# A down projection taken from six groups of matmuls to seven block products, with the sums of its blocks formed in DRAM

## The chip, the cores and the metric

The kernel runs on one core of a Trainium2 chip (a core has TensorE, here PE; VectorE, DVE; ScalarE, ACT; GpSimd, POOL; and SyncE, SP, which only issues transfers). The metric is device time in microseconds, the median of the runs of one program.

## What is computed

Two layers of an encoder over 1024 tokens of width 1024: a mixer of three parallel head groups, a cross-attention to a memory of 256 tokens, and a gated feed-forward part of width 2816. Only the last is changed in what it multiplies:

```python
def conv_gated_ffn(h, w_up, conv_w, conv_b, w_down):
    a = h @ w_up
    ap = jnp.pad(a, ((0, 0), (1, 1), (0, 0)))
    a = ap[:, :-2] * conv_w[0] + ap[:, 1:-1] * conv_w[1] + ap[:, 2:] * conv_w[2] + conv_b
    gate, val = a[..., :D_FF], a[..., D_FF:]
    return (jax.nn.silu(gate) * val) @ w_down

for l in range(DEPTH):                       # DEPTH = 2
    x = x + hybrid_mixer(rms_norm(x, mix_norm[l]), ...)
    x = x + memory_cross_attention(rms_norm(x, mem_x_norm[l]), mem, ...)
    x = x + conv_gated_ffn(rms_norm(x, ffn_norm[l]), ffn_w_up[l], ffn_conv_w[l], ffn_conv_b[l], ffn_w_down[l])
return rms_norm(x, final_norm)
```

## The kernel before

The residual x stays in SBUF as eight tiles of 128 tokens. A product in float32 accuracy is three matmuls: each operand is split into a high part, rounded to the format that PE multiplies, and a low part, the rest, and high x high, high x low and low x high go into one bank of PSUM (`mm3`, L113 to L115). PSUM is eight banks: four single ones (`bank`) and two pairs (`pair`). SBUF beside x is 46 slots of 128 x 1024 words (`s` in the rows).

**Attention.** An item is one head and one half of the queries: 4 steps of scores, exponentials on ACT (L296), scaling by the sum on POOL (`scale`, L302), then transposes on PE (L137) whose results ACT and DVE split (L120, L121), then the product with the values. There are 24 items in a layer, and the transposes of one stand among the scores of the next.

**The up projection's sums of blocks.** The up projection already is seven products of blocks in place of eight. The sums of weight blocks that it needs are formed in DRAM during the attention: a copy of one block (`up_copy`, issued on ACT, L778) and, four items later, a transfer that adds another block to it (`up_add`, issued on POOL, L781). Two of the four sums add an earlier sum. 24 copies and 24 adds a layer are spread over 20 items. In the rows these tensors are `u`.

**The up projection.** 22 channel tiles j, seven products each of 12 matmuls (L1104 to L1106). A weight piece of 256 KB is fetched nine products ahead (L1050) and split four ahead (L1057 on ACT, L1058 on DVE). The gate and value of j then pass a convolution (L1144 to L1152) and are multiplied (`gate`, L1158); `keep` stores the tile of 128 channels x 1024 tokens to DRAM (L1162, tensor `g`).

**The down projection.** The 22 channel tiles are read back in six groups of 3, 4, 4, 4, 4, 3. `load_down` fetches the weight rows and the stored tile through SP (L103), takes the high parts on POOL (L107, weights) and ACT (L105, activations) and the low parts on DVE (L108). For each group, token tile and half of the 1024 output columns there is one bank with 3 matmuls for each channel tile, and DVE adds it to x (`add_to_x`, L366). In the last group the next layer's norm of each token tile follows (L142, L128, L129, L144), and the transposes of its first half of the tokens stand between the last tiles; at the end of the second layer the final norm and the output (L1272, L1274; `final_last` for the last tile, L1251 to L1264).

**The order.** The functions are called in the order of the code, and the framework places each engine's instructions from it by its own estimates of when buffers come free; an engine then executes its list strictly in that order. Calls under `tc.keep_in_program_order` stay where the code has them. A tile of PSUM can be taken only when the one before it in the same bank has had its last reader.

## Time and profile before

| | us |
|---|---|
| median of 3 runs | 2869.32 (2869.23 to 2872.6) |
| the profiled execution, its own time | 2875.77 |
| its span, first to last instruction | 2873.6 |
| PE busy in it | 2798.3 |
| mean granted clock | 0.994 |

The page of the profile tells busy time by engine, groups of instructions by line with the mean of one in nanoseconds, and transfers by queue. Where a row has `x1297 | 509.1, 392`, there were 1297 instructions, busy for 509.1 us, 392 ns each; what follows names the idle time before them and what ended it. The matmuls overlap each other, so a record of 392 ns is not the time that one costs.

### The profile page before, as it was taken

To read this page: it belongs to the slowest core of one execution; us is meant where nothing else is said; L and a number is where in the kernel's file an instruction comes from. 1 tells how busy PE (TensorE), PEld (TensorE's weight loads), DVE (VectorE), ACT (ScalarE), POOL (GpSimd) and SP (SyncE) were. 2 spreads that over 40 slices of the span, in tenths; PEclk is the share of its full clock that TensorE was granted. 3 is DMA by queue.
4 is the path that set the end of the run, shared out by engine and by line. 5 is a ranking of instruction groups with operands and counts; after the bars stand their busy time and mean duration, and the time that the engine had idled before them with its cause. 6 is when DMAs were issued, how large, how long until landed. Compare 5 with 4: busy or idle time off the path is not lost. (4 is left out here: it accounts for less than half of the span.)

```text
span 2873.6 us, 37125 instructions
## 1 busy us (share of the span) xinstructions
PE 2798.3 (97%) x13909; PEld 2344.1 (82%) x13909; DVE 1975.6 (69%) x2825; ACT 1341.3 (47%) x2572; POOL 660.9 (23%) x628
## 2 busy tenths in 40 slices
PE   9998999999999999999999989999999999999998
PEld 7987787788878888888889777878887888888887
DVE  5578888656687777864445788895667877778544
ACT  4377877224554444310133778772345544443101
POOL 3244566320000000210123345663200000002100
PEclk9999999999999999999999999999999999999999
DMA  4015676311133333531110157752221333335311
GB/s 145 23 51 131 170 176 133 88 61 64 45 110 132 122 121 131 183 133 51 38 46 23 60 135 178 175 130 66 68 65 45 125 122 122 131 126 189 110 59 59
DMA packets 93635, 297.61 MB, mean 104 GB/s; under 512 B 10384, under 2 KB 11024, under 8 KB 83216
## 3 DMA queue, kind: packets, MB, share of 16 engines
q1 hardware_dynamic: 79488, 202.70, 21.1%
q0 software_dynamic: 6912, 46.14, 8.8%
q10 hardware_dynamic: 7056, 46.40, 4.5%
q8 instruction: 110, 1.80, 0.2%
q14 instruction: 69, 0.57, 0.1%
HBM read 267.94 MB, written 119.54 MB: 135 GB/s over the span
## 5 line engine op out<-in xcount | busy, mean ns | idle before, releaser
L113 PE MATMUL bank<-s,s 128*128 128x512 f32 (+4 forms) x1831 | 678.8, 371 | 5.9 <-DVE s L124 2.6
L115 PE MATMUL bank<-s,s 128*128 128x512 f32 (+4 forms) x1831 | 676.1, 369 | 0.9 <-DVE s L124 0.5
L114 PE MATMUL bank<-s,s 128*128 128x512 f32 (+4 forms) x1831 | 674.3, 368 | 0.0
L107 POOL TENSOR_SCALAR s<-s 128x1024 fp32r<-128x1024 f32 (+1 forms) x114 | 142.8, 1257 | 1374.3 <-DMA s<-in_w_down 1007.7
L121 DVE TENSOR_TENSOR s<-bank,s 128x512 fp32r<-128x512 f32 (+3 forms) x552 | 332.7, 631 | 109.1 <-ACT s L120 106.8
L120 ACT ACTIVATE s<-bank 128x512 fp32r<-128x512 f32 (+3 forms) x552 | 288.3, 555 | 238.4 <-PE bank L137 165.8
L113 PEld LDWEIGHTS bank<-s,s 128*128 128x128 f32 x1831 | 345.5, 189 | 62.7 <-DVE s L121 3.7
L115 PEld LDWEIGHTS bank<-s,s 128*128 128x128 f32 x1831 | 346.2, 189 | 53.8 <-DVE s L124 1.6
L114 PEld LDWEIGHTS bank<-s,s 128*128 128x128 f32 x1831 | 346.3, 189 | 50.9
L137 PE MATMUL bank<-ident,s 128*128 128x128 f32 (+1 forms) x2320 | 327.8, 276 | 45.5 <-DVE s L121 37.0
L137 PEld LDWEIGHTS bank<-ident,s 128*128 128x128 f32 (+1 forms) x2320 | 271.6, 141 | 108.0 <-issue 32.6
L302 POOL TENSOR_SCALAR s<-s,stat 128x1024 f32<-128x1024 f32 x192 | 224.5, 1169 | 249.1 <-DVE stat L301 159.6
L366 DVE TENSOR_TENSOR x<-x,bank 128x512 f32<-128x512 f32 x214 | 145.6, 683 | 195.5 <-PE bank L115 195.1
L292 DVE TENSOR_REDUCE stat<-pair 128x1 f32<-128x1024 f32 x192 | 234.2, 1220 | 65.4 <-PE pair L734 38.0
L1105 PE MATMUL bank<-s,s 128*128 128x512 f32 x704 | 274.8, 390 | 0.9 <-DVE s L206 0.9
L1106 PE MATMUL bank<-s,s 128*128 128x512 f32 x704 | 274.2, 389 | 0.0
L1104 PE MATMUL bank<-s,s 128*128 128x512 f32 x704 | 274.0, 390 | 0.0
L1057 ACT ACTIVATE s<-s 128x512 fp32r<-128x512 f32 x308 | 187.9, 627 | 161.7 <-PE bank L1106 49.8
L108 DVE TENSOR_TENSOR s<-s,s 128x1024 fp32r<-128x1024 f32 (+4 forms) x172 | 217.4, 1274 | 59.8 <-POOL s L107 46.1
L296 ACT ACTIVATE s<-pair,stat 128x1024 f32<-128x1024 f32 x192 | 214.3, 1116 | 16.9 <-DVE stat L292 10.3
L1058 DVE TENSOR_TENSOR s<-s,s 128x512 fp32r<-128x512 f32 x308 | 201.3, 687 | 24.4 <-ACT s L1057 20.8
L1104 PE MATMUL pair<-s,s 128*128 128x512 f32 x528 | 208.5, 395 | 1.2 <-ACT s L208 1.0
(164 smaller groups left out, 4519.5 us busy)
## 6 DMA issues: line engine op xcount, KB each, us to landing
s<-u SPq DMA_DIRECT2D x176, 256.0 KB, 3.0
u<-in_w_up ACTq DMA_DIRECT2D x40, 1024.0 KB, 6.5
s<-in_w_up SPq DMA_DIRECT2D x132, 256.0 KB, 3.3
g<-s SPq DMA_DIRECT2D x44, 512.0 KB, 2.8
s<-in_w_down SPq DMA_DIRECT2D x44, 512.0 KB, 4.4
s<-g SPq DMA_DIRECT2D x44, 512.0 KB, 5.4
u<-in_w_up POOLq DMA_DIRECT2D x20, 1024.0 KB, 9.8
u<-u POOLq DMA_DIRECT2D x20, 1024.0 KB, 10.0
```

The costliest lines, as they stand in the source:

```text
L108: nc.vector.tensor_tensor(lo[:, :cols], raw[:, :cols], f(hi[:, :cols]), ALU.subtract)
L113: nc.tensor.matmul(o, l[0], r[0], start=first, stop=False)
L114: nc.tensor.matmul(o, l[0], r[1], start=False, stop=False)
L115: nc.tensor.matmul(o, l[1], r[0], start=False, stop=last)
L120: nc.scalar.activation(hi, src, AF.Copy)
L121: nc.vector.tensor_tensor(lo, src, f(hi), ALU.subtract)
L137: nc.tensor.transpose(b[:m, j * P : (j + 1) * P], s, ident)
L292: nc.vector.reduce_max(self.nm[:, 0:1], s, axis=AX.X, negate=True)
L302: nc.gpsimd.tensor_scalar(p, p, r[:, 0:1], 0.0, ALU.mult, ALU.add)
L1104: nc.tensor.matmul(o, lh, rh, start=k == 0 and m in (1, 5, 6), stop=False, skip_group_check=True)
L1105: nc.tensor.matmul(o, lh, rl, start=False, stop=False, skip_group_check=True)
L1106: nc.tensor.matmul(o, ll, rh, start=False, stop=k == 3, skip_group_check=True)
```

## The change

The down projection becomes seven products of blocks too. The two halves of the tokens, the two halves of the output columns, and even and odd channel tiles make blocks of 512 tokens x 1408 channels and 1408 channels x 512 columns. A product runs over all 11 channel tiles of its block in four banks, one for each token tile, and DVE adds or subtracts the four results to one quarter of x when the product ends, some of them after a further product was accumulated in the same bank. The order is 1, 5, 6, 3, 7, 2, 4; products 1, 6, 7 and 4 use the four single banks, from the first to the last without release, and 5, 3 and then 2 the two pairs.

The sums of weight blocks are formed as the up projection's, in the same 20 items: 36 copies and 36 adds a layer in place of 24. The sums of the activations' blocks are formed in DRAM as well: for a pair of channel tiles `keep` issues seven stores of 256 KB on SP and four adds on POOL. Each block of a product fetches one activation piece and one weight piece of 256 KB (L1194, L1195 of the changed kernel), and takes both high parts on ACT and both low parts on DVE.

The copies move from ACT's queue to SP's, and each is made to wait for the scaling on POOL that stands last before it in the code (`Item.last`), so that they don't all start at once. The last four blocks of product 4 are done tile by tile, so that norms or output can follow.

```diff
-FGROUPS = [3, 4, 4, 4, 4, 3]
+D_AHEAD, D_FETCH = 4, 8
+UP_PARTS, DOWN_PARTS = (2, 4, 4, 4, 4, 4), (3, 4, 4)
...
-            nc.gpsimd.tensor_scalar(p, p, r[:, 0:1], 0.0, ALU.mult, ALU.add)
+            Item.last = nc.gpsimd.tensor_scalar(p, p, r[:, 0:1], 0.0, ALU.mult, ALU.add)
...
-        def up_copy(m, i):
-            tc.keep_in_program_order(nc.scalar.dma_start(up_sum[m, i], up_piece({5: 2, 6: 0, 7: 0, 3: 1}[m], i)))
...
+            def copy(self, m, i):
+                c = nc.sync.dma_start(self.sum[m, i], self.piece({5: 2, 6: 0, 7: 0, 3: 1}[m], i))
+                tc.add_manual_dep(ins_of(c), ins_of(Item.last).name, mybir.DependencyInfo(mybir.DependencyClass.Sync, mybir.DependencyReason.DATA), reason="not sooner")
+
+            def add(self, m, i):
+                src = self.sum[{6: 5, 3: 6}[m], i] if m in (6, 3) else self.piece({5: 3, 7: 2}[m], i)
+                tc.keep_in_program_order(nc.gpsimd.dma_start(self.sum[m, i], src, accum_op=ALU.add))
...
+        w_u = Blocks([a["w_up"][l, b] for b in range(4)], UP_PARTS, "u")
+        w_d = Blocks([a["w_down"][l, b] for b in range(4)], DOWN_PARTS, "d")
...
-            extra.setdefault(n * 5 // 6, []).append(lambda m=m, i=i: up_copy(m, i))
-            extra.setdefault(n * 5 // 6 + 4, []).append(lambda m=m, i=i: up_add(m, i))
+        extra, steps = {}, w_u.steps() + w_d.steps()
+        for n, (w, m, i) in enumerate(steps):
+            g = n * 20 // len(steps)
+            extra.setdefault(g, []).append(lambda w=w, m=m, i=i: w.copy(m, i))
+            extra.setdefault(g + 4, []).append(lambda w=w, m=m, i=i: w.add(m, i))
...
         def gate(j):
             z = st[j]
-            nc.vector.tensor_tensor(z["cg"], z["cg"], z["cv"], ALU.mult)
+            for i in range(2):
+                c, v = quarter(z["cg"], i), quarter(z["cv"], i)
+                if i == j % 2:
+                    nc.vector.scalar_tensor_tensor(c, c, -1.0, v, ALU.mult, ALU.mult)
+                else:
+                    nc.vector.tensor_tensor(c, c, v, ALU.mult)
             sl.put(z["cv"])
 
         def keep(j):
-            nc.sync.dma_start(gd[j], st[j]["cg"])
-            sl.put(st.pop(j)["cg"])
+            z, i = st.pop(j)["cg"], j // 2
+            for q, h in ((("21", 1), ("u4", 1), ("22", 0), ("u2", 0)) if j % 2 else (("11", 1), ("u1", 0), ("u3", 0))):
+                nc.sync.dma_start(gq[q, i], quarter(z, h))
+            sl.put(z)
+            for q, p in ((("u3", "22"), ("u2", "u1"), ("u4", "u2")) if j % 2 else (("u1", "11"),)):
+                nc.gpsimd.dma_start(gq[q, i], gq[p, i], accum_op=ALU.add)
+
+        NP = NF // 2
+        d_order = [(m, i) for m in (1, 5, 6, 3, 7, 2, 4) for i in range(NP)]
...
+        def make_d():
+            if (mi := next(d_make, None)) is not None:
+                z, ops = d_raw.pop(mi), (sl.get(), sl.get())
+                d_op[mi] = ops
+                for q in range(2):
+                    src, hi, lo = quarter(z, q), quarter(ops[q], 0), quarter(ops[q], 1)
...
+                        nc.scalar.activation(hi, src, AF.Copy)
+                        nc.vector.tensor_tensor(lo, src, f(hi), ALU.subtract)
...
+        def d_mm(m, i, t, o, c0=0, n=CH):
+            g, w = (tuple(quarter(z, h) for h in range(2)) for z in d_op[m, i])
+            lh, rh = tok(g, t), cols(w, c0, n)
+            for k, (p, q) in enumerate(((0, 0), (0, 1), (1, 0))):
+                nc.tensor.matmul(o, lh[p], rh[q], start=m in (1, 5, 2) and i == 0 and k == 0, stop=i == NP - 1 and k == 2, skip_group_check=True)
...
+        def down(after0, after1, tail):
+            for m, i in d_order:
+                fetch_d()
+                make_d()
...
+                if m == 4 and i >= NP - D_AHEAD:
+                    if i == NP - 1:
+                        for t in range(TPC):
+                            if tail and t == TPC - 1:
+                                tail(bs[t])
+                                break
+                            for k in range(NP - D_AHEAD, NP):
+                                d_mm(m, k, t, bs[t])
+                            d_add(m, t)
+                            after1(TPC + t)
...
+                for t in range(TPC):
+                    d_mm(m, i, t, bs[t])
...
+                if i == NP - 1:
+                    for t in range(TPC):
+                        d_add(m, t)
+                        if m == 7:
+                            after0(t)
...
+        def first_half(t):
+            nt.rows(t)
+            if t == TPC - 1:
+                todo.extend(lambda k=k: nt.turn(0, range(k, k + 1)) if k >= 0 else None for n in range(KT) for k in (n, -1, -1, -1))
```

The code asks for the next layer's transposes (`nt.turn`) already during product 2; where they stand on PE the framework decides.

Where the order of the instructions moves, in three places. First POOL in the first layer's attention, where the adds to sums (DMA rows; `u_6_2<-u_5_2` adds sum 5 of the third part to sum 6) stand among the scalings (L302, in the changed kernel L305). Before:

```order
L781 DMA u_6_2_1629<-u_5_2_1623 128x2048
L234 TENSOR_TENSOR s_348_3938<-s_142_1698,s_73_703 128x128
L302 TENSOR_SCALAR s_340_3850<-s_340_3850,stat 128x1024
L236 TENSOR_TENSOR s_348_3938<-s_142_1698,s_73_703 128x128
L302 TENSOR_SCALAR s_343_3894<-s_343_3894,stat 128x1024
L671 TENSOR_TENSOR s_318_3651<-s_318_3651,s_344_3900 128x1024
L302 TENSOR_SCALAR s_347_3932<-s_347_3932,stat 128x1024
L325 TENSOR_TENSOR s_352_3979<-s_353_3980 64x512
L302 TENSOR_SCALAR s_351_3973<-s_351_3973,stat 128x1024
L781 DMA u_6_3_1630<-u_5_3_1624 128x2048
L781 DMA u_7_3_1636<-in_w_up 128x2048
```

and in the changed kernel:

```order
L782 DMA u_6_2_1629<-u_5_2_1623 128x2048
L782 DMA u_6_3_1630<-u_5_3_1624 128x2048
L305 TENSOR_SCALAR s_291_3390<-s_291_3390,stat 128x1024
L305 TENSOR_SCALAR s_294_3435<-s_294_3435,stat 128x1024
L305 TENSOR_SCALAR s_297_3468<-s_297_3468,stat 128x1024
L328 TENSOR_TENSOR s_287_3351<-s_303_3515 64x512
L305 TENSOR_SCALAR s_302_3509<-s_302_3509,stat 128x1024
L782 DMA u_7_3_1636<-in_w_up 128x2048
L782 DMA u_3_2_1641<-u_6_2_1629 128x2048
```

Most items now carry two adds, and `u_3_2`, which reads sum `u_6_2`, stands one item behind the add that forms it.

Second SP ahead of the attention's end. Before, the loads of w_out follow the loads ahead of the attention directly:

```order
L103 DMA s_123_1596<-in_w_uq 128x576
L103 DMA s_129_1608<-in_w_ukv 128x768
L103 DMA s_126_1602<-in_w_uq 128x576
L103 DMA s_527_5701<-in_w_out 128x1024
L103 DMA s_539_5850<-in_w_out 128x1024
```

In the changed kernel all 36 copies of the layer stand between them; these are the last four:

```order
L777 DMA d_5_2_1647<-in_w_down 128x2048
L777 DMA d_7_2_1653<-in_w_down 128x2048
L777 DMA d_6_2_1650<-in_w_down 128x2048
L777 DMA d_3_2_1656<-in_w_down 128x2048
L106 DMA s_527_5737<-in_w_out 128x1024
L106 DMA s_539_5886<-in_w_out 128x1024
```

Third PE at the end of the first layer's down projection, where the transposes (L137, in the changed kernel L140) of the next layer's first half stand. Before, twelve of them come together between matmuls of the last group:

```order
L113 MATMUL bank<-s_1162_12142,s_1165_12176 128x512
L114 MATMUL bank<-s_1163_12143,s_1165_12176 128x512
L115 MATMUL bank<-s_1162_12142,s_1166_12177 128x512
L137 MATMUL bank<-ident,s_1167_12259 128x128
L137 MATMUL bank<-ident,s_1168_12289 128x128
L137 MATMUL bank<-ident,s_1169_12319 128x128
L137 MATMUL bank<-ident,s_1170_12349 128x128
L137 MATMUL bank<-ident,s_1167_12259 128x128
L137 MATMUL bank<-ident,s_1168_12289 128x128
```

In the changed kernel they come four at a time among the last tiles of product 4 (L1223):

```order
L1223 MATMUL bank<-s_1277_12738,s_1276_12737 128x512 x3
L140 MATMUL bank<-ident,s_1216_12339 128x128
L140 MATMUL bank<-ident,s_1217_12348 128x128
L140 MATMUL bank<-ident,s_1218_12357 128x128
L140 MATMUL bank<-ident,s_1219_12366 128x128
L1223 MATMUL bank<-s_1281_12765,s_1280_12764 128x512
L140 MATMUL bank<-ident,s_1216_12339 128x128
L140 MATMUL bank<-ident,s_1217_12348 128x128
L140 MATMUL bank<-ident,s_1218_12357 128x128
L140 MATMUL bank<-ident,s_1219_12366 128x128
```

None of them stands ahead of the last four blocks.

More of the change, by code (lines that the diff above doesn't have):

```diff
@@ L379, in project_to_x @@
                 after(t)
-    def norm_after(nt):
-        def after(t):
-            nt.rows(t)
-            if t >= 5:
-                nt.turn(0, [range(0, 3), range(3, 6), range(6, 8)][t - 5])
-        return after
     def layer(l, nt, last):
@@ L451, in layer @@
             gm_cols(0)
-            nt.turn(1, range(0, 1))
             gm_cols(1)
-            nt.turn(1, range(1, 4))
+            nt.turn(1, range(0, 4))
             gm_cols(2)
@@ L780, in up_add @@
-        def up_add(m, i):
-            tc.keep_in_program_order(nc.gpsimd.dma_start(up_sum[m, i], {5: lambda: up_piece(3, i), 6: lambda: up_sum[5, i], 7: lambda: up_piece(2, i), 3: lambda: up_sum[6, i]}[m](), accum_op=ALU.add))
-        def up_block(m, j):
-            if m in (1, 2, 4):
-                return a["w_up"][l, {1: 0, 2: 1, 4: 3}[m]][:, j * CH : (j + 1) * CH]
-            i = max(i for i in range(len(UP_PARTS)) if up_at[i] <= j)
-            return up_sum[m, i][:, (j - up_at[i]) * CH : (j - up_at[i] + 1) * CH]
@@ L1038, in layer @@
         wop, fetched, made = {}, iter(order), iter(order)
-        gd = [dpool.tile([P, S], F32, tag=f"g{l}_{j}", name=f"g{l}_{j}") for j in range(NF)]
         raws, half = {}, []
@@ L1049, in fetch @@
                 raws[jm] = half.pop(0)
-                nc.sync.dma_start(raws[jm][0], up_block(jm[1], jm[0]))
+                nc.sync.dma_start(raws[jm][0], w_u.block(jm[1], jm[0]))
         def make_w():
@@ L1182, in down @@
-        def down(i, after=None, tail=None):
-            gs, wd = ready.pop(i)
-            if i + 1 < len(groups):
-                todo.extend(load_down(i + 1))
-            def then(t):
-                for _ in range(-(-len(todo) // (NT - t))):
-                    todo.popleft()()
-                if after:
-                    after(t)
-            project_to_x(gs, wd, len(gs), then, 0, NT - 1 if tail else NT)
-            if tail:
-                tail(gs, wd, len(gs))
-            put2(wd + gs)
+            z, i = st.pop(j)["cg"], j // 2
@@ new lines, in fetch_d @@
+        def fetch_d():
+            if (mi := next(d_fetch, None)) is not None:
+                m, i = mi
+                z = d_raw[mi] = sl.get(F32)
+                nc.sync.dma_start(quarter(z, 0), gq[{1: "11", 2: "21", 3: "22", 4: "u4", 5: "u1", 6: "u2", 7: "u3"}[m], i])
+                nc.sync.dma_start(quarter(z, 1), w_d.block(m, i))
+        def make_d():
[4 more added lines that the diff above has]
+                    src, hi, lo = quarter(z, q), quarter(ops[q], 0), quarter(ops[q], 1)
+                    if q == 0 and mi[0] in (2, 6):
+                        nc.scalar.activation(hi, src, AF.Copy, scale=-1.0)
+                        nc.vector.scalar_tensor_tensor(lo, src, -1.0, f(hi), ALU.mult, ALU.subtract)
+                    else:
+                        nc.scalar.activation(hi, src, AF.Copy)
+                        nc.vector.tensor_tensor(lo, src, f(hi), ALU.subtract)
+                sl.put(z)
@@ new lines, in d_banks @@
+        def d_banks(m):
+            if m == 1:
+                d_bank["p"] = [bank() for _ in range(TPC)]
+            if m in (5, 2):
+                d_bank["q"] = [quarter(b, i) for b in (pair(), pair()) for i in range(2)]
+            return d_bank["p" if m in (1, 6, 7, 4) else "q"]
+        def d_mm(m, i, t, o, c0=0, n=CH):
[3 more added lines that the diff above has]
+                nc.tensor.matmul(o, lh[p], rh[q], start=m in (1, 5, 2) and i == 0 and k == 0, stop=i == NP - 1 and k == 2, skip_group_check=True)
@@ L1231, in layer @@
             return None
         nt = NormT(colts[l + 1][:, C_MIX : C_MIX + 8])
-        down(len(groups) - 1, after=norm_after(nt))
+        def first_half(t):
+            nt.rows(t)
+            if t == TPC - 1:
+                todo.extend(lambda k=k: nt.turn(0, range(k, k + 1)) if k >= 0 else None for n in range(KT) for k in (n, -1, -1, -1))
+        down(first_half, nt.rows, None)
+        while todo:
+            todo.popleft()()
         return nt
```

115 lines of the change are left out of this document (67 added, 48 removed).

## The prediction

> **What bounds the kernel now.** I read part 1 of the page, then what PE waited for, then busy time by stretches. First the engines over the whole span, and the longest of PE's waits (microseconds in all, times, longest).
>
> ```profile
> PE 2798.3 (97%) x13909; PEld 2344.1 (82%) x13909; DVE 1975.6 (69%) x2825; ACT 1341.3 (47%) x2572; POOL 660.9 (23%) x628
> PE bank L137 <- DVE s L121: 37.0, 36, 2.6
> ```
>
> PE is busy for 2798 of 2874 us, and its longest wait, in which the attention's transposes wait for a bank, is 37 us in all. The table by stretches (busy us of PE, PEld, DVE, ACT, POOL; then clock, DMA share, GB/s) shows where there is slack: six stretches of the first layer's attention, then its up projection, then its down projection.
>
> ```profile
> 180.00:240.00 60.00, 54.68 (x326) 45.03 (x324) 46.78 (x76) 50.33 (x116) 24.46 (x22) 1.00 0.24 77
> 240.00:300.00 60.00, 53.46 (x298) 43.68 (x299) 50.47 (x96) 46.65 (x96) 29.38 (x29) 0.97 0.59 146
> 300.00:360.00 60.00, 56.71 (x323) 46.79 (x322) 51.79 (x86) 52.19 (x106) 34.00 (x34) 1.00 0.72 177
> 360.00:420.00 60.00, 57.67 (x325) 48.16 (x324) 49.03 (x86) 47.61 (x97) 35.43 (x34) 0.97 0.70 176
> 420.00:480.00 60.00, 56.31 (x318) 45.80 (x317) 51.48 (x85) 46.30 (x84) 39.48 (x39) 1.00 0.71 159
> 480.00:540.00 60.00, 57.56 (x309) 46.76 (x309) 51.24 (x71) 33.76 (x62) 35.31 (x29) 1.00 0.37 88
> 795.00:1190.00 395.00, 393.50 (x1724) 322.57 (x1725) 297.48 (x370) 184.36 (x254) 2.10 (x2) 1.00 0.37 123
> 1205.00:1425.00 220.00, 219.87 (x968) 181.08 (x967) 112.24 (x136) 22.25 (x25) 28.45 (x23) 1.00 0.25 86
> ```
>
> In the down projection PE idles 0.1 us of 220, while DVE works half the time and the DMA engines a quarter: there the time is the number of matmuls. In attention PE idles 24 of 360 us, with ACT and DVE at 56 to 87% and the DMA engines at 0.7 of their time: little is free there.
>
> **The matmuls removed.** A busy PE is not a pace, so I take it from starts: two matmuls of the first layer's down projection, 56 apart, and the first and last start of the adds to x.
>
> ```profile
> 1249.64 0.39 PE L114 MATMUL bank<-s,s 128*128 128x512 f32 x1
> 1262.34 0.39 PE L113 MATMUL bank<-s,s 128*128 128x512 f32 x1
> L366 DVE TENSOR_TENSOR x<-x,bank x96: 673/686/689, 1205.5 to 1443.6; 128x512 f32<-128x512 f32 x96
> ```
>
> 12.70/56 = 0.2268 us each, although each record is 0.39 us long: they overlap. Before, a layer has 8 token tiles x 2 halves x 22 channel tiles x 3 = 1056 of them, by this pace 239.5 us (the adds run over 238). After, it has 7 products x 11 blocks x 4 token tiles x 3 = 924. The difference of 132, times 0.2268, is 29.9 us a layer, **59.9 us** in all. The last tile's smaller pieces hold the same columns and cost the same. All else is what gives some of this back.
>
> **Attention: the copies leave ACT, and there are more of them.** First an issue on ACT and adds on POOL (min/median/max ns), all adds' time to landing, three queues with MB and share of 16 engines, and two adds one item apart.
>
> ```profile
> L778 ACTq DMA_DIRECT2D u<-in_w_up x48: 497/498/635, 177.2 to 1878.2; - x48
> L781 POOL DMA_DIRECT2D u<-u x24: 762/808/1128, 264.3 to 1938.3; - x24
> DMA to landing us min/median/max: 5.1/9.5/15.4
> q1 hardware_dynamic: 79488, 202.70, 21.1%
> q0 software_dynamic: 6912, 46.14, 8.8%
> q10 hardware_dynamic: 7056, 46.40, 4.5%
> 264.28 0.81 POOL L781 DMA_DIRECT2D u<-u  x1
> 278.25 0.79 POOL L781 DMA_DIRECT2D u<-u  x1
> ```
>
> ACT gets rid of 24 x 0.498 = 12 us a layer. How much of PE's idle time hangs on it no row shows; it lies between 0 and those 12 us. ACT has room between most evictions, so I take 2 us a layer: **-4**.
>
> Against it stand half as many transfers again. The copies took 4.5% of 2873.6 us for 46.40 MB, 2.79 us of all engines per MB; the adds 5.48. An item lasts 14.0 us, and copies and adds of 1.05 MB now come 1.8 to the item in place of 1.2: 1.8 x 1.05 x 8.27 = 15.6 us of transfers in 14.0, where it was 10.4 (0.74; the rows show 0.70 to 0.72). With the true sizes, items 4 to 21 ask for 251 us of transfers in 252. They fit, with a backlog of up to 13 us on the way. Copies may be late, since each add comes four items behind its copy. But an add that reads an earlier sum waits on POOL's queue, and seven in a layer now stand one item behind the add that they need. Behind such an add POOL holds the scaling of the probabilities, for which the transposes on PE wait. At 9.5 us to landing nothing waits; at 10 to 15 us plus backlog some wait 1 to 5 us, and a turn follows its scaling by about a step (3.5 us), which hides part. Bounds: nothing, and 13 us a layer (the whole backlog); POOL's 12 more issues, 10 us in 360 with POOL 41 to 66% busy, lie inside. I take 3 us a layer, nearer to the measured landing: **+6**.
>
> The Trainium skill (DMA: Bandwidth & Descriptors, Anatomy of one DMA) fits a transfer from GpSimd at 2.0 us plus its bytes over 436 GB/s. By it a 1 MB add would take 4.4 us and hold the engines for an estimated 2.4, and this term would be 0. The trace disagrees: these adds, which read both their sides, land after a median of 9.5 us, and the measurement decides.
>
> The copies wait in SP's queue. Behind them there stand only loads of w_out, needed from item 23 on; the last copy is freed in item 19: nothing.
>
> **Up projection.** PE's waits and SP's longest there:
>
> ```profile
> PE pair L1105 <- DVE s L209: 0.9, 2, 0.7
> SPq L1162 <- DVE s L1158: 100.3, 20, 13.8
> ```
>
> A pair of channel tiles takes 14 products x 12 x 0.2268 = 38 us. It now stores seven pieces of 256 KB in place of two of 512 KB, and has four adds of 256 KB on POOL, which is idle there (2.1 us in 395). By the prices above (q1: 2.99 us per MB) that is 0.8 x 2.99 + 1.05 x 5.48 = 8 us of transfers more in 38, 0.37 going to 0.58. The fetches behind a store that waits for its gate stand five products (13.6 us) ahead of their use, and even the longest wait of 13.8 us cost PE nearly nothing. Bounds 0 and 10 (one such wait in four uncovered); **+1**.
>
> **Down projection.** What a product of one block needs: evictions to two halves on ACT and DVE, two fetches; and the densest transfers of the trace.
>
> ```profile
> L1057 ACT ACTIVATE s<-s 128x512 fp32r<-128x512 f32 x308 | 187.9, 627 | 161.7 <-PE bank L1106 49.8 <-DVE s L1158 41.2 <-PE pair L1106 35.6
> L1058 DVE TENSOR_TENSOR s<-s,s 128x512 fp32r<-128x512 f32 x308 | 201.3, 687 | 24.4 <-ACT s L1057 20.8
> s<-u SPq DMA_DIRECT2D x176, 256.0 KB, 3.0
> 2600.00:2640.00 40.00, 40.00 (x177) 32.90 (x176) 34.08 (x34) 16.87 (x18) 11.97 (x10) 1.00 0.73 258
> ```
>
> PE takes 12 x 0.2268 = 2.72 us a block. ACT needs 2 x 0.627 = 1.25, DVE 2 x 0.687 plus 28 adds of 0.686 spread over 77 blocks = 1.62, the transfers 0.524 MB x 2.99 = 1.57 (0.58 of the engines, 193 GB/s, where 258 has been seen). Every one is under 2.72, and a fetch has four blocks, 10.9 us, to land in 3.0. So the stage stays PE's: 0. The banks alternate between bank and pair tiles, so no add holds up the next product. At its start DVE is nearly full (34.1 of 40 us in the last row) with the last convolutions and the first splits together: 0 to 4 us a layer, I take 1: **+2**.
>
> **Between the layers.** The products hold all four single banks until their last four blocks, so the 32 transposes for the next layer's first half, which stood between matmuls of the last group, now squeeze in among the last tiles. Rows of DVE work in 1425 to 1450, and PE's transposes there:
>
> ```profile
> L366 DVE TENSOR_TENSOR x<-x,bank 128x512 f32<-128x512 f32 x9 | 6.0, 679 | 0.0
> L124 DVE SCALAR_TENSOR_TENSOR s<-bank,cols,s 128x512 fp32r<-128x512 f32 x8 | 5.8, 746 | 1.1 <-ACT s L123 1.1
> L144 DVE TENSOR_SCALAR s<-x,stat 128x1024 f32<-128x1024 f32 x6 | 5.3, 885 | 2.0 <-POOL stat L129 1.8
> L128 DVE TENSOR_SCALAR stat<-stat 128x1 f32<-128x1 f32 x5 | 0.8, 153 | 3.1 <-ACT s L142 3.1
> 1432.34 1.47 PE L137 MATMUL bank<-ident,s 128*128 128x128 f32 x12
> 1433.57 0.48 PE L113 MATMUL bank<-s,s 128*128 128x512 f32 x1
> ```
>
> After the first tile DVE must do 4 adds, 8 splits, 4 rows: 4 x 0.679 + 8 x 0.746 + 4 x (0.885 + 0.153) = 12.8 us. PE has 36 matmuls and 32 transposes of 1.23/12 = 0.10 us: 11.4 us. It waits for the difference and for the first add: **+3**, between 0 and 12.8 (none of it hidden).
>
> **The end.** The last row tile's output follows on DVE behind tile 6's:
>
> ```profile
> 2862.12 0.70 DVE x L366
> 2863.96 0.28 PE L113 MATMUL bank<-s,s 128*128 128x256 f32 x1
> 2865.99 0.28 PE L115 MATMUL bank<-s,s 128*128 128x256 f32 x1
> 2864.84 1.29 DVE L1274 SCALAR_TENSOR_TENSOR s<-x,stat,s 128x1024 f32<-128x1024 f32 x1
> 2866.65 0.75 DVE L1251 TENSOR_TENSOR x<-x,bank 128x256 f32<-128x256 f32 x2
> ```
>
> The matmuls of 256 columns start 2.03/17 = 0.119 us apart. Tile 7 had 9 of 0.227 and 18 of 0.119, 4.2 us of PE; now it has 24 of 0.119, 2.9 us. L1274 ends 4.0 us after tile 6's last add began, so the last add comes about **+0.5** later behind PE's end.
>
> **Sum.** -59.9 - 4 + 6 + 1 + 2 + 3 + 0.5 = -51.4. The profiled execution took 2875.77 us (2873.6 of span, 2.2 around it), 6.45 above the median of the runs, 2869.32. Taken off the median: **2818 us**, in a profiled execution about 2824.
>
> **Rivals.** *The sums' transfers become attention's bound* (slower). For it: shares of 0.7, and adds that need each other one item apart; against it: 251 us fit in 252 at the measured price. It decides once they cost over 1.1 times that under load; at 1.12 POOL waits out 30 us a layer, PE with it: 2818 - 6 + 60 = 2872. *Late fetches in the down projection*: twice the transfers of before, two to a block, on one queue behind stores. If each block loses 0.15 us, 154 x 0.15 = 23: 2841. For it speaks that landing grows with load (adds 5.1 to 15.4 us); against it the 10.9 us of lead. *ACT was what attention waited for*: then the 24 us come off whole and POOL costs nothing: 2818 - 20 - 6 = 2792. ACT at 77 to 87% up to 480 us speaks for it; the waits named for PE end on DVE.
>
> **Chances.** The forecast (2800 to 2836) 0.68; late fetches, or a part of the POOL waits (2836 to 2863) 0.17; ACT's gain 0.08; no change 0.02; slower 0.05. Leaving out ACT's case and the top tenth gives 2800 to 2846. Within 0.2% (5.7 us) is what a measurement here cannot tell from no change: faster 0.93, same 0.02, slower 0.05.
>
> **What would show it.** 1860 matmuls of the down projection, starting 0.227 us apart; each down stage some 210 us long; PE idle no more than 1 us per 100 in it. A semaphore wait on POOL's adds in attention well over 15 us in all would show the first rival; PE waiting for the splits' fetches the second; PE's idle time in 180 to 540 falling from 24 to under 15 us the third. The forecast is wrong if the pace of 0.227 doesn't hold, or if PE's idle time outside the down projection grows by over 20 us.

## The result: 0.983 of the time before, by two errors that cancelled

The changed kernel takes 2821.94 us (median of 4 runs, 2819.99 to 2823.89), the kernel before in the same series 2869.28: the ratio is 0.9833, with a 95% interval of 0.9816 to 0.985. The forecast was 2818 (2800 to 2846). The medians differ by 47.3 us, the spans of the profiled executions by 51.9, since that of the kernel before lay 6.45 above its median and that of the changed one 1.9 above its own. Times of kernels here are medians of their executions, without one of the first experiment's kernel, which took 9880.91 us at a granted clock of 0.486.

The profile after, first the page's row on PE and the groups of the new down projection (busy us, mean ns; then the first and last start of the same matmuls):

```profile
PE 2743.0 (97%) x13648; PEld 2296.2 (81%) x13648; DVE 1966.1 (70%) x2953; ACT 1468.0 (52%) x2836; POOL 691.8 (25%) x696
L1223 PE MATMUL bank<-s,s 128*128 128x512 f32 (+1 forms) x1068 | 242.7, 387 | 1.6 <-DVE stat L131 1.6
L1223 PE MATMUL pair<-s,s 128*128 128x512 f32 x792 | 180.5, 389 | 0.0
L1223 PE MATMUL bank<-s,s x1068: 278/389/486, 1201.6 to 2814.6; 128*128 128x512 f32 x174, 128*128 128x256 f32 x4
L1223 PE MATMUL pair<-s,s x792: 389/389/390, 1231.5 to 2782.5; 128*128 128x512 f32 x198
```

There are 1068 + 792 = 1860 matmuls, as forecast. Product 1, 132 of them, runs from 1201.6 to the first one into a pair at 1231.5: 29.9/132 = 0.2265 us each, the pace that the prediction took.

The stretches that answer to those shown of before (busy us of PE, PEld, DVE, ACT, POOL; clock, DMA share, GB/s):

```profile
180.00:240.00 60.00, 59.30 (x358) 49.96 (x357) 51.42 (x89) 53.40 (x121) 25.96 (x23) 1.00 0.42 129
240.00:300.00 60.00, 57.62 (x331) 46.69 (x330) 55.58 (x102) 52.03 (x104) 38.12 (x38) 1.00 1.00 256
300.00:360.00 60.00, 56.06 (x310) 44.36 (x309) 49.86 (x87) 49.72 (x101) 37.32 (x37) 1.00 1.02 247
360.00:420.00 60.00, 58.30 (x326) 48.39 (x325) 48.24 (x87) 46.74 (x97) 36.47 (x35) 0.97 1.02 252
420.00:480.00 60.00, 49.22 (x255) 40.19 (x256) 42.20 (x65) 38.16 (x70) 32.51 (x33) 0.89 0.88 210
480.00:540.00 60.00, 58.07 (x307) 47.57 (x306) 49.72 (x68) 33.41 (x60) 37.13 (x31) 0.97 0.46 108
795.00:1190.00 395.00, 393.54 (x1725) 322.95 (x1726) 297.13 (x388) 185.77 (x259) 32.86 (x40) 1.00 0.61 172
1240.00:1400.00 160.00, 160.00 (x708) 132.53 (x707) 80.21 (x125) 59.51 (x102) 6.09 (x7) 1.00 0.48 155
```

The up and the down projection are as forecast: PE loses 1.5 us of 395 in the one, nothing of 160 in the other. Attention is another matter. PE's idle time from 180 to 540 us is 21 us, nearly the 24 of before, but it lies elsewhere: PE does more in the first stretches (358 and 331 matmuls and transposes on record, where it was 326 and 298) and loses 10.8 us in one stretch, 420 to 480, behind 180 us in which the DMA engines were full (shares of 1.00 to 1.02). Idle time is not all that a wait costs: the mean granted clock of the first attention is 0.97 here (173 to 519 us) and was 0.99 before (174 to 520 us), by these rounded shares an estimated 7 us of 346. So a little less idle time of PE is not less time here.

From the timelines of POOL and PE come the starts that bound the stages; the table has each stage's length in us.

| stage | before | after | difference |
|---|---|---|---|
| start to the first scaling, layer 0 | 173.8 | 173.7 | -0.1 |
| first to last scaling (attention), layer 0 | 345.7 | 344.9 | -0.8 |
| to the first product of the up projection | 252.6 | 253.5 | +0.9 |
| up projection's products | 427.7 | 429.3 | +1.6 |
| last up product to the first scaling of layer 1 | 400.1 | 373.3 | -26.8 |
| attention, layer 1 | 345.0 | 344.9 | -0.1 |
| to the first up product | 252.1 | 254.3 | +2.2 |
| up projection's products | 429.4 | 429.1 | -0.3 |
| last up product to PE's end | 239.9 | 211.8 | -28.1 |
| PE's end to the end of the span | 7.3 | 6.9 | -0.4 |

Their sum is -51.9, which is the difference of the spans, 2873.6 and 2821.7. So attention as a whole gained and lost nothing. Inside it this is what happened: the start of the first scaling of an item, in the first layer, in us after the first scaling of item 0.

| item | before | after | difference |
|---|---|---|---|
| 5 | 71.8 | 64.0 | -7.8 |
| 10 | 141.1 | 127.7 | -13.4 |
| 15 | 213.9 | 200.6 | -13.3 |
| 17 | 244.8 | 230.6 | -14.2 |
| 18 | 258.6 | 249.8 | -8.8 |
| 20 | 291.3 | 279.6 | -11.7 |
| 21 | 304.8 | 302.4 | -2.4 |
| last scaling | 345.7 | 344.9 | -0.8 |

By item 10 the changed kernel is 13 us ahead; in the second layer it is 12.5 by item 10 and 12.3 by item 17. It keeps that while the DMA engines are full, loses some around item 18 and most of the rest between items 20 and 21. That place can be read in POOL's timeline (start, us, and in brackets the idle time before it and what ended it) and in PE's:

```profile
454.40 0.69 POOL L685 TENSOR_SCALAR s<-s,cols 128x512 fp32r<-128x512 f32 x1
464.46 1.05 POOL L110 TENSOR_SCALAR s<-s 128x1024 fp32r<-128x1024 f32 x1 [9.38 <-DMA s<-in_w_out]
466.95 1.12 POOL L305 TENSOR_SCALAR s<-s,stat 128x1024 f32<-128x1024 f32 x1
465.37 0.27 PE L140 MATMUL bank<-ident,s 128*128 128x128 f32 x1
468.13 0.33 PE L140 MATMUL bank<-ident,s 128*128 128x128 f32 x1 [2.49 <-POOL s L305]
469.89 0.48 PE L140 MATMUL bank<-ident,s 128*128 128x128 f32 x1 [1.43 <-POOL s L305]
474.24 0.90 PE L140 MATMUL bank<-ident,s 128*128 128x128 f32 x3 [3.87 <-DVE s L127]
```

POOL stands for 9.4 us before the rounding of the first weights of w_out (L110). The scalings of the probabilities (L305) are behind it, and the transposes on PE (L140) wait for these; PE's last wait, 3.87 us for DVE, comes the same way, since DVE had itself stood 7.22 us for the product behind them on POOL (L685). The load itself took, from issue to landing, 19.2 us; in the kernel before the load at this place took 5.6 (issues between 440 and 470 us of the changed kernel, and 450 and 475 of the kernel before):

```profile
s<-in_w_out SPq DMA_DIRECT2D x1, 512.0 KB, 19.2
```

```profile
s<-in_w_out SPq DMA_DIRECT2D x1, 512.0 KB, 5.6
```

It was issued at 445 us in the one and at 454 in the other, so SP's queue did not make it late; the full engines did. The second layer shows the same wait, 7.5 us long. The adds' landing grew too, from a median of 9.5 us to 17.5, and POOL waited before them (all of L782 in both layers: idle us, times, by what ended it; then landing):

```profile
  DVE s L124: 18.5, 7
  DVE stat L304: 6.9, 3
  DVE stat L295: 5.3, 1
  DMA u<-in_w_up: 3.3, 4
  DMA u<-u: 2.3, 2
DMA to landing us min/median/max: 7.8/17.5/25.6
```

An add reads and writes DRAM alone, so DVE is named here only because its event came last by the record. In all it is some 36 us of POOL's time, 18 a layer. In the kernel before POOL waits before no add at all.

The issue and landing times of the adds in the trace tell more. In each of these waits three earlier adds were still under way when POOL was free to go on, and the add was issued 0.3 to 0.4 us after the oldest of them had landed: the one at 340.64 us, behind 5.17 us of waiting, 0.31 us after a landing at 340.33. In none of the traces of this case is an add issued while more than two earlier ones are under way. About half of the waiting, 18.6 us in seven waits, stands before adds that read no earlier sum. So POOL stands when adds land too slowly for their number, and not only when an add needs the one before it. Where this limit comes from no run shows.

So there were two theories to test. **The prediction's:** leaving ACT's queue is worth 2 us a layer, the added transfers cost 3, w_out's loads nothing. **The trace's:** the move off ACT is worth 13 us or more a layer, and full DMA engines take it back, through w_out's load (9 us) and through adds on POOL.

### The profile page after: what moved, and what is told of

It reads as the page before. It is cut to its first block, busy times and chain, and to the rows that moved or that the text cites. A ratio compares the mean times of both kernels' runs of the same rounds, so it can differ in the third digit from the quotient of the medians.

```text
span 2821.7 us, 38000 instructions
## 1 busy us (share of the span) xinstructions
PE 2743.0 (97%) x13648; PEld 2296.2 (81%) x13648; DVE 1966.1 (70%) x2953; ACT 1468.0 (52%) x2836; POOL 691.8 (25%) x696
## 3 DMA queue, kind: packets, MB, share of 16 engines
q0 software_dynamic: 23040, 92.28, 18.2%
## 4 chain that ended last, share of the span: by engine, by line
PE 79%; DVE 7%; POOL 4%; issue 4%; ACT 4%; DMA 1%; SPq 0%; POOLq 0%; DVEq 0%; ACTq 0%
PE bank L1223 8%; PE bank L116 7%; PE bank L118 7%; PE bank L117 7%; PE pair L1223 6%; PE bank L1111 5%; PE bank L1112 5%; PE bank L140 5%; PE bank L1110 5%; PE pair L1110 4%; PE pair L1111 4%; PE pair L1112 4%; PE bank L318 2%; PE bank L319 2%; PE pair L116 2%
## 5 line engine op out<-in xcount | busy, mean ns | idle before, releaser
L116 PE MATMUL bank<-s,s 128*128 128x512 f32 (+4 forms) x1124 | 403.6, 360 | 9.7 <-DVE s L124 4.3
L118 PE MATMUL bank<-s,s 128*128 128x512 f32 (+4 forms) x1124 | 400.2, 356 | 2.4 <-DVE s L111 1.4
L117 PE MATMUL bank<-s,s 128*128 128x512 f32 (+4 forms) x1124 | 399.2, 355 | 0.0
L140 PE MATMUL bank<-ident,s 128*128 128x128 f32 (+1 forms) x2320 | 333.3, 277 | 40.7 <-POOL s L305 15.9
L140 PEld LDWEIGHTS bank<-ident,s 128*128 128x128 f32 (+1 forms) x2320 | 274.6, 141 | 105.7 <-POOL s L305 21.3
L1063 ACT ACTIVATE s<-s 128x512 fp32r<-128x512 f32 x308 | 187.9, 628 | 168.8 <-PE bank L1112 49.8
L305 POOL TENSOR_SCALAR s<-s,stat 128x1024 f32<-128x1024 f32 x192 | 231.0, 1215 | 175.7 <-DVE stat L304 125.1
L295 DVE TENSOR_REDUCE stat<-pair 128x1 f32<-128x1024 f32 x192 | 233.7, 1217 | 47.9 <-PE pair L118 24.8
L132 POOL TENSOR_TENSOR stat<-stat,mhalf 128x1 f32<-128x1 f32 (+3 forms) x94 | 86.3, 918 | 646.8 <-DVE stat L131 646.4
L116 PEld LDWEIGHTS bank<-s,s 128*128 128x128 f32 x1124 | 212.2, 189 | 39.6 <-DVE s L124 5.1
L1223 PE MATMUL bank<-s,s 128*128 128x512 f32 (+1 forms) x1068 | 242.7, 387 | 1.6 <-DVE stat L131 1.6
L1208 DVE TENSOR_TENSOR s<-s,s 128x512 fp32r<-128x512 f32 x264 | 170.6, 685 | 93.1 <-ACT s L1207 92.2
L118 PEld LDWEIGHTS bank<-s,s 128*128 128x128 f32 x1124 | 212.4, 189 | 27.5 <-DVE s L111 1.9
L1223 PEld LDWEIGHTS bank<-s,s 128*128 128x128 f32 x1068 | 198.7, 188 | 42.3 <-DVE stat L131 1.8
L117 PEld LDWEIGHTS bank<-s,s 128*128 128x128 f32 x1124 | 212.6, 189 | 23.9 <-DVE s L111 0.2
L1207 ACT ACTIVATE s<-s 128x512 fp32r<-128x512 f32 x264 | 153.5, 624 | 142.1 <-DMA s<-g_u 42.5
## 6 DMA issues: line engine op xcount, KB each, us to landing
u<-in_w_up SPq DMA_DIRECT2D x40, 1024.0 KB, 13.3
```

What stands on the lines that cost most here:

```text
L116: nc.tensor.matmul(o, l[0], r[0], start=first, stop=False)
L117: nc.tensor.matmul(o, l[0], r[1], start=False, stop=False)
L118: nc.tensor.matmul(o, l[1], r[0], start=False, stop=last)
L140: nc.tensor.transpose(b[:m, j * P : (j + 1) * P], s, ident)
L295: nc.vector.reduce_max(self.nm[:, 0:1], s, axis=AX.X, negate=True)
L305: Item.last = nc.gpsimd.tensor_scalar(p, p, r[:, 0:1], 0.0, ALU.mult, ALU.add)
```

## Experiments

Ratios are to the kernel before, with 95% intervals. "Attention" is the time from the first to the last scaling of a layer, first and second layer; it was 345.7 and 345.0 before, 344.9 and 344.9 after.

### The copies back on ACT

```diff
-                c = nc.sync.dma_start(self.sum[m, i], ...)
-                tc.add_manual_dep(ins_of(c), ins_of(Item.last).name, ...)
+                tc.keep_in_program_order(nc.scalar.dma_start(self.sum[m, i], ...))
```

> The changed kernel with its 36 copies a layer issued on ACT again, in program order, with no semaphore; all else as changed. By the prediction's term (ACT's issues cost attention 2 us a layer) the time grows by 3 times that, for 18 us of issues in place of 12: 2822 + 6 = 2828. If the 13 us a layer that the changed kernel is ahead by item 10 of attention come from ACT's queue, that lead is gone, and the scaling of item 10 comes as late as in the kernel before (142 us after the first): 2835 to 2850. If the lead comes from something else, 2822.

2832.17 us, ratio 0.9868 (0.9853 to 0.9883); attention 350.1 and 349.7. The scaling of item 10 comes 141.1 us after the first one, to the tenth what it was before, and not 127.7: the lead comes from the move of the copies. The time is 3 us under the range that this theory gave (2835 to 2850); POOL's longest wait for w_out is 5.5 us here in place of 9.4, which may be why.

### That part of the change alone

```diff
-            tc.keep_in_program_order(nc.scalar.dma_start(up_sum[m, i], ...))
+            c = nc.sync.dma_start(up_sum[m, i], ...)
+            tc.add_manual_dep(ins_of(c), ins_of(Item.last).name, ...)
```

> The kernel before with one part of the change alone: its 24 copies a layer go to SP's queue, each held for the scaling ahead of it. By the prediction's term 2869 - 4 = 2865. If ACT's queue was what attention waited for, 11 to 14 us a layer come off by item 10 and stay off to the end, since the transfers stay at 0.7 of the engines: 2869 - 26 = 2843, and PE's idle time from 180 to 540 us falls from 24 to 11 us. If the lead of the changed kernel has another source (its other spacing of the copies), 2869.

2837.93 us, ratio 0.9888 (0.9875 to 0.9902): 33 us off the median, and 37.9 off the profiled span, for a part that the prediction priced at 4. Attention takes 325.0 and 327.7 us, 20.7 and 17.3 less, and more than the 26 in all that was expected if ACT's queue was the cause. Three of its stretches:

```profile
180.00:240.00 60.00, 59.31 (x360) 50.12 (x359) 51.12 (x88) 53.37 (x122) 26.25 (x24) 1.00 0.30 90
360.00:420.00 60.00, 59.79 (x345) 50.04 (x345) 51.43 (x91) 49.93 (x103) 41.35 (x40) 1.00 0.78 184
420.00:480.00 60.00, 59.40 (x341) 49.16 (x341) 55.77 (x89) 49.50 (x90) 39.69 (x38) 1.00 0.66 150
```

PE is busy for 59.3 to 59.8 of 60 us, with the DMA engines at 0.3 to 0.8 of their time. PE's longest wait from 180 to 540 us, the transposes' for a bank that DVE's low parts set free, was this in the kernel before (us in all, times, longest)

```profile
PE bank L137 <- DVE s L121: 18.6, 18, 2.5
```

and is this with the copies on SP:

```profile
PE bank L140 <- DVE s L124: 2.2, 5, 0.9
```

### Is it the time of the issues on ACT?

17 to 21 us a layer is more than the 12 us that 24 issues last. So this run keeps the copies on SP and puts a small transfer on ACT in each one's place.

```diff
+            s = dpool.tile([P, 16], F32, ...)
+            tc.keep_in_program_order(nc.scalar.dma_start(s, up_piece(...)[:, :16]))
```

> The kernel before with its copies on SP, held (325 and 328 us from the first to the last scaling), plus at the place of each copy one transfer of 8 KB that nothing reads, issued on ACT in program order: 24 issues a layer on ACT as in the kernel before, without their bytes. If the time of the issues on ACT is what the copies cost attention there (17 to 21 us a layer), it goes back to about 345 us a layer, 2872. If it is the order that the framework makes when the large copies are ACT's (PE's order here is nearly that with the copies on SP), it stays at 325 to 333 us, 2838 to 2850.

2834.0 us, ratio 0.9879 (0.9866 to 0.9893); attention 329.1 and 324.8. The issues cost nothing that can be seen. Three rows of the kernel before show why: between two evictions on ACT stands an issue of 0.50 us, and they start 0.49 us apart, where two without one take 1.09 together.

```profile
305.02 0.60 ACT L120 ACTIVATE s<-bank 128x512 fp32r<-128x512 f32 x1
305.19 0.50 ACTq L778 DMA_DIRECT2D u<-in_w_up  x1
305.51 0.59 ACT L120 ACTIVATE s<-bank 128x512 fp32r<-128x512 f32 x1
307.08 1.09 ACT L120 ACTIVATE s<-bank 128x512 fp32r<-128x512 f32 x2
```

The order of the instructions stayed nearly that of the run with the copies on SP: DVE's list in the first attention agrees with it in 94% of its records, and in 67% with that of the kernel before. So what is left is either the large copies' traffic on ACT's queue, or the order that the framework makes when it has them on ACT. The two runs that follow leave issues, bytes and queues of the kernel before as they are, and ask for copies and adds one step earlier or later in the item, so that only the order differs, and with it the moment of each copy.

```diff
-            if s == 2 and g < n:
+            if s == 1 and g < n:        # the second run: s == 3
```

> The kernel before, with its copies and adds asked for one step earlier in each item (after the second step of scores, not the third). Issues, bytes and queues are the same, only the framework's order of the instructions differs. If ACT's queue by itself (issues, transfers of a megabyte on it) costs attention 17 to 21 us a layer, attention stays at 343 to 348 us and the time at 2870. If it is the order that the framework makes around the copies, attention moves by over 5 us a layer, in one direction or the other.

> The same one step later (after the fourth step of scores). Again: 343 to 348 us of attention and 2870 if ACT's queue costs it; another time by over 5 us a layer if the framework's order does.

One step earlier: 2895.99 us, ratio 1.0082 (1.0068 to 1.0096), attention 353.0 and 353.7. One step later: 2870.68, ratio 0.9999 (0.999 to 1.0008), attention 340.0 and 339.3, but the stage behind it is 3.6 and 2.8 us longer. Between these two the order by itself moves attention by 13.0 and 14.4 us, at the same issues and bytes. So the order can be worth this much. None of the three orders with large copies on ACT reaches 325, and no run here has ACT's traffic without ACT's order, so the remaining 12 to 15 us are not separated by a run.

The traces speak for the order. The wait named above, PE's transposes for DVE's low parts, is in us, first and second attention (180 to 540 and 1590 to 1935 us):

| kernel | first | second |
|---|---|---|
| before | 18.6 | 17.2 |
| copies back on ACT | 21.1 | 21.5 |
| one step earlier | 20.9 | 20.9 |
| one step later | 8.7 | 8.1 |
| copies on SP | 2.2 | 2.2 |
| the same with small issues on ACT | 1.6 | 1.6 |

Between the kernel before and that with the copies on SP this wait differs by 16.4 and 15.0 us, most of the 20.7 and 17.3. No DMA ends it, and DVE's instructions are not slower beside the copies (the maximum over 1024 scores takes 1220 and 1217 ns). What differs is where DVE's list has the low parts. DVE waits for scores before these maxima for 28.2 us in the kernel before (180 to 500 us) and for 17.2 us with the copies on SP, and low parts that stand behind such a maximum in its list wait with it. Why the framework makes this order is not shown.

### w_out's loads at their place

```diff
-            w_o[n, u] = load(a["w_out"][l, n, u], 1024)
+            w_o[n, u] = load(a["w_out"][l, n, u], 1024, pin=n == 0)
...
+            if pin:                              # in load, for the rounding on POOL
+                tc.keep_in_program_order(h)
```

> The changed kernel with the first four loads of w_out rounded on POOL where the code has them (item 23), not where the framework's order put the first of them (item 20). By the prediction (loads of w_out cost nothing) 2822. If POOL's 9.4 us of waiting for that load, which lands after 19.2 us on full DMA engines, is what takes back attention's lead at items 20 to 21, it is gone: 2822 - 2 x 9 = 2804, and the scaling of item 21 stays 9 to 12 us ahead of the kernel before. If POOL then waits as long elsewhere (an add, a later load), 2815 to 2822.

2808.96 us, ratio 0.9779 (0.9765 to 0.9792): 13 us less than the changed kernel, attention 338.2 and 335.8. Attention is 6.7 and 9.1 us shorter, and the stretch where PE was busy for 49.2 us has 54.3:

```profile
420.00:480.00 60.00, 54.29 (x292) 43.77 (x291) 47.30 (x76) 43.36 (x78) 35.54 (x36) 0.94 0.95 228
```

So w_out's loads, where the framework had put their rounding, were not free. It was less than expected: item 21 is 4.8 and 7.5 us ahead of the kernel before, not 9 to 12, and POOL still waits 6.5 us for such loads in the first layer. An edit here also changes the framework's order, which by itself moved attention by more than this, so the size is less sure than the wait that went away. Some 11 us a layer above the run with the copies' move alone are still there.

### Adds farther from the sums that they read

```diff
-                return [(self, m, i + o) for i in range(0, n, 2) for m, o in ((5, 0), (5, 1), (7, 0), ...) if i + o < n]
+                return [(self, m, i) for m in (5, 7, 6, 3) for i in range(n)]
```

> The changed kernel with w_out's loads rounded at their place, and the 36 steps of a layer in another order: all of sum 5, then 7, then 6, then 3, so that an add stands 1.7 to 6.7 items behind the sum that it reads, where most stood one or two. Copies, adds and bytes are the same. Attention took 338 and 336 us with w_out's loads at their place, 325 and 328 with 24 copies and adds. If POOL waits behind adds for the sums that they read (the prediction's step), attention falls to 326 to 331 us and the time from 2809 to about 2793. If full engines hold attention up in another way (copies that land late, the adds' own landing), it stays at 334 to 338: 2803 to 2809.

With w_out's loads at their place: 2803.07 us, ratio 0.9762 (0.9748 to 0.9777); attention 329.5 and 333.8, so 8.7 us less in the first layer and 2.0 in the second. POOL's idle time before adds falls from 37.3 us to 29.5, and all of it, 12 waits, again stands where three earlier adds were under way, with no add nearer than 1.7 items to the sum that it reads. So the nearness of adds that need each other is not what POOL mainly waits for. The median landing is still 17.5 us here. Whether the gain in attention comes from the waits that went or from the framework's other order is not separated; the two layers gained unlike amounts.

### The copies without the semaphore

```diff
-                c = nc.sync.dma_start(self.sum[m, i], ...)
-                tc.add_manual_dep(ins_of(c), ins_of(Item.last).name, ...)
+                nc.sync.dma_start(self.sum[m, i], ...)
```

> The changed kernel without the semaphore: its 72 copies stay on SP's queue and wait for nothing. The framework's order puts the copies of both layers among the first loads of layer 0. 2 x 34.7 MB at 2.79 us a MB are 194 us of all DMA engines there. If that makes the loads of w_kv, w_q and w_a late, layer 0's attention starts 50 to 150 us later than at 174 us, and the second layer's attention, which keeps only its adds, takes 326 us in place of 345: 2850 to 2950. If the hold isn't needed, the start stays at 174 us and both attentions gain: 2785 to 2800.

2799.71 us in two executions, ratio 0.9755 (0.9738 to 0.9773). The time is that of the second case, but not quite as it had it: the start does suffer, by 10.7 us (first scaling at 184.4), and both attentions gain more than that, to 330.4 and 328.0. In the stretch before the first scaling the engines are full and PE waits for weights (the wait's row is of the whole span; its longest, 11.2 us, is the one here, with ACT standing 10.97 us for a load of w_ukv):

```profile
120.00:180.00 60.00, 48.16 (x261) 46.71 (x259) 39.29 (x47) 22.92 (x77) 26.78 (x13) 0.91 1.00 318
PE bank L116 <- ACT s L126: 12.0, 2, 11.2
```

All 36 adds of a layer are still in attention here, and it takes 5.4 and 0.3 us more than with 24. POOL waits 1.7 us before adds, in place of 36. So the adds alone were not dear; copies and adds in the same 20 items were. The semaphore, which holds the copies back until then, costs 22 us more than it saves.

### w_down's sums formed later

```diff
-        extra, steps = {}, w_u.steps() + w_d.steps()
+        extra, steps, d_steps = {}, w_u.steps(), w_d.steps()
...
             if i < len(seq):                     # the cross-attention to the memory
                 m_score(*seq[i])
+                for w, m, n in d_steps[i * 12 // 8 : (i + 1) * 12 // 8]:
+                    w.copy(m, n)                 # held for a scaling in m_score
...
             post(j, m)                           # the up projection
+            if i >= 8 and i % 8 == 0 and i // 8 <= len(d_steps):
+                w, dm, dn = d_steps[i // 8 - 1]
+                w.add(dm, dn)
```

> The changed kernel with the sums of w_down's blocks formed later: their 12 copies a layer during the cross-attention to the memory, each held for a scaling there, and their 12 adds during the up projection; attention keeps 24 copies and 24 adds. By the prediction's term (adds and transfers cost 3 us a layer) 2822 - 6 = 2816. If full DMA engines cost attention the late load of w_out (9 us a layer) and waits behind adds (4 us), both go: 2822 - 26 = 2796, with the DMA share in attention back at 0.7. If the added transfers press the up projection (0.61 of the engines now, 0.8 then), up to 10 us of that come back: 2806.

2788.75 us, ratio 0.9713 (0.97 to 0.9726): 33 us less than the changed kernel. Attention takes 328.4 and 325.9 us, what the copies' move alone gave. The up projection carries the adds and stays as long as it was (429.7 and 429.5 us), with its DMA share up from 0.61 to 0.78:

```profile
420.00:480.00 60.00, 58.91 (x336) 48.13 (x336) 55.54 (x87) 49.57 (x90) 38.88 (x38) 1.00 0.67 152
795.00:1190.00 395.00, 393.38 (x1727) 323.03 (x1726) 295.84 (x386) 189.38 (x267) 43.30 (x53) 1.00 0.78 213
```

Without this third of the transfers attention thus has back all that it had lost. POOL waits before no add in attention. The edit gives the framework another order too, but attention comes out within 3.4 us of the copies' move alone in either layer.

### And the transposes between the layers

```diff
+        def turn2(self, c, k0):
+            z = pair()
+            for n, k in enumerate((k0, k0 + 1)):
+                ...                              # as turn, into the two halves of z
...
-                todo.extend(lambda k=k: nt.turn(0, range(k, k + 1)) if k >= 0 else None for n in range(KT) for k in (n, -1, -1, -1))
+                todo.extend([lambda: None] * (2 * NP))
+                todo.extend(lambda k=k: nt.turn2(0, k) if k >= 0 else None for n in range(0, KT, 2) for k in (n, -1, -1, -1))
```

> The kernel with w_down's sums formed after attention, and the next layer's transposes of its first half written into the two pairs, which are free from the end of product 2 on, so that they stand inside product 4 and not behind it. If the 3 us that the changed kernel loses between the layers come from the single banks that product 4 holds, the way from the last up product of layer 0 to the first scaling of layer 1 falls from 373 to 370 us and the time from 2789 to 2786. If the norms set it, nothing changes: 2789.

2783.81 us, ratio 0.97 (0.9687 to 0.9713). From the last up product of layer 0 to the first scaling of layer 1 it takes 369.1 us in place of 373.1: 4 us, one more than expected, and PE's waits between the layers fall from 3.0 us in the changed kernel to 0.6, so the single banks held by product 4 were what cost time there. The whole gained 5 us, though its interval overlaps that of the run without it.

> As the run with both edits, and w_out's loads rounded at their place in the code as well. In the changed kernel that was worth 13 us, because the load landed after 19.2 us on full engines. Here it lands after 3.6 us: if only the full engines made the place matter, nothing is left to gain, 2786; if POOL's waits for it (13.5 us in 4) still reach PE, up to 4 us a layer, 2778.

2779.97 us, ratio 0.969 (0.9676 to 0.9703). This is the shortest of all kernels here, 42 us below the changed one and 90 below the one before, but 4 us from the run without w_out's part, with intervals that overlap: whether that edit still does anything is open. The way from the last up product of layer 0 to the first scaling of layer 1 takes 370.1 us here.

## Why the forecast's number was right, point by point

The stages of the table are read from one profiled execution of each kernel; by the medians the copies' move took 33 us in place of 38.

| term | forecast | measured | from |
|---|---|---|---|
| matmuls removed | -59.9 | together -55.3 with the next three | stages |
| start of the down projection | +2, 1 a layer | +1.8 in the second layer; in the first 3.1 together with the next | 29.9 - 28.1; 29.9 - 26.8 |
| between the layers | +3 | +3 to +4 | 373.1 to 369.1 and 370.1 without it |
| the end | +0.5 | -0.4 | 7.3 to 6.9 |
| up projection | +1 | +1.3 | stages |
| copies leave ACT | -4 | -38.0 | attention, the move alone |
| more copies and adds in attention | +6 | +37.1 in all | attention, after less the move alone |
| of this: w_out's loads | 0 | +15.8, order included | loads at their place |
| attention to up projection | 0 | +3.1 | stages |

**The down projection** was forecast right for the reasons given: the pace held (0.2265), its PE is busy for 160 of 160 us, the transfers and splits are hidden. The start and the wait between the layers were sized within about 1 us, and the run with the transposes in the pairs shows that the reason given for the latter, the held single banks, is it.

**The term -4 failed.** The step "it lies between 0 and those 12 us" took ACT's share to be the time of the issues. Issues of the same number cost nothing, and the move was worth 17 to 21 us a layer, more than the bound. The term left out that the order of the instructions on PE, ACT and DVE changes with the queue that the copies are on: 15 to 16 us a layer of the gain is PE's wait for DVE's low parts, the very wait that the prediction had found to be PE's longest, 37.0 us, and had not tied to the copies. Order alone moved attention by 13 and 14 us a layer between two other places of the same copies.

**The term +6 failed the other way.** The transfers' demand was right: 251 us forecast for 252, and the measured share is 1.00 to 1.02 for 180 us on end; the adds' price held (18.2% of 2821.7 us for 92.28 MB, 5.6 us per MB). What was wrong is "at 9.5 us to landing nothing waits", and above all "needed from item 23 on ... nothing" on w_out. Its load landed in 5.6 us in the kernel before, and in 19.2 where the engines were full; and the framework had put its rounding on POOL between items 20 and 21. The rest, 37.1 - 15.8 = 21.3 us in both layers, lies inside the 26 that the prediction gave as its bound for the adds, but its reason was only half of it: POOL waited as long before adds that read no earlier sum, whenever three were under way. How much of the 21.3 us are these waits and how much is order is open.

**The rivals** had both been described, and both came true together in their size: ACT's case (forecast 2792 if alone; the move alone took 33 us off the kernel before) and that of the sums' transfers (2872 if alone). Neither came true in its mechanism: it was not ACT's time for issues, and not a price of transfers 1.1 times as high. Their sum, about nothing, stood near the forecast's +2 by chance. The sign named for the transfers, POOL waiting before adds for well over 15 us, was there (36 us); that for ACT, PE's idle time under 15 us, was hidden by the other.

The fit of the Trainium skill for a transfer from GpSimd (DMA: Bandwidth & Descriptors, Anatomy of one DMA), by which an add of 1 MB would take an estimated 4.4 us, is off by more here than in the kernel before: the adds landed after a median of 17.5 us.

Left open: a run that separates order from the traffic on ACT's queue in the 17 to 21 us of the copies' move, where the traces speak for order, and the 3 us between attention and up projection, which no run was made for.

## What to carry to other kernels

When a change asks for transfers in a stage where the DMA engines come to a full share, price not only its own transfers but every load that lands in that stretch, and look in the order of each engine that is behind such a load: the cost comes out there. A copy that is moved to another queue may change the order that a framework gives the other engines, which can be worth more than the issue; take one part of the change alone and compare the progress within the stage, item by item, since a gain and a loss in it cancel in its total. Work that is needed late belongs in a stage whose engines have room, here 33 us for moving a third of the sums.

## What was not expected of the hardware

Landing times grew far more than the DMA share. From 0.7 to a full share, the adds' median went from 9.5 to 17.5 us, and the load of w_out from 5.6 to 19.2. And POOL issued no add while three earlier ones were under way, in any trace here, so adds that land late stop POOL itself.

PE came back slowly from the wait. In 20 us with 7.8 us of idle time the granted clock is 0.74 (0.50 from 470 to 479 us), and in 40 us before 0.96:

```profile
460.00:480.00 20.00, 12.21 (x55) 9.69 (x54) 11.35 (x17) 7.35 (x14) 10.30 (x11) 0.74 0.59 120
420.00:460.00 40.00, 37.01 (x202) 30.49 (x203) 30.85 (x50) 30.82 (x56) 22.21 (x22) 0.96 1.03 254
475.37 0.63 PE L319 MATMUL bank<-s,s 128*128 128x512 f32 x1
475.79 0.63 PE L318 MATMUL bank<-s,s 128*128 128x512 f32 x1
```

The two matmuls behind the wait start 0.42 us apart and last 0.63 us each, where the down projection's start 0.2265 apart and last 0.39.
